# Two tile pools in place of one, the last operand pair built in steps, activations loaded by POOL's queue

## The chip, the cores and the metric

One core of a Trainium2 chip runs the whole program in one launch. The metric is device microseconds of that core, as the median of several runs. A profiled execution of the same kernel gives a trace; a difference of 0.2% (4.3 us here) is about what a measurement of this kernel can tell from no change.

## The reference

The program computes a small hybrid encoder on x of 1024 positions by 1024 channels in float32. It has two mixer layers, each followed by a gated feed-forward layer (FFN) of width 2816, and a last RMSNorm:

```python
for l in range(DEPTH):                       # DEPTH = 2
    h = rmsnorm(x, g_mix[l])
    if l % 2 == 0:                           # even mixer
        xa, ga, hb, bg, cg = jnp.split(h @ w_in_even[e], SPLIT_EVEN, axis=-1)
        xa = causal_dwconv(xa, lru_conv_w[e]) + lru_conv_b[e]
        ya = rg_lru(xa, ...) * jax.nn.gelu(ga)
        yb = bg * causal_dwconv(cg * hb, sconv_w[e])
        x = x + jnp.concatenate([ya, yb], axis=-1) @ w_out_even[e]
    else:                                    # odd mixer: pooling and HGRN2
        ...
        x = x + jnp.concatenate([yc, yd], axis=-1) @ w_out_odd[o]
    h = rmsnorm(x, g_ffn[l])
    u = causal_dwconv(h @ ffn_w_up[l], ffn_conv_w[l]) + ffn_conv_b[l]
    x = x + (jax.nn.gelu(u) * (h @ ffn_w_gate[l])) @ ffn_w_down[l]
return rmsnorm(x, g_final)
```

## The kernel before

**Numbers.** Every float32 operand of a large product is split into two parts that TensorE takes (`split`, L120: ScalarE, called ACT in the profile, writes the high part, VectorE, called DVE, the low part). Each product is then three matmuls: high·high, high·low, low·high. Channels lie on the 128 partitions, positions in the free dimension, so x is eight tiles of 128x1024 (512 KB).

**Stages.** The head (L644 to L696) loads x and the first weights channel block by channel block, multiplies them as they come, and takes the squares for the norm. `norm_cols` (L183) turns the sum of squares `ss` into a reciprocal root per position: eight small matmuls `pst`, a POOL power. `norm_bcast` (L196) spreads it over the partitions: DVE `dg`, the split `dh`, four matmuls `psb`, and the tile `rb`. The even mixer then runs 17 blocks of 48 matmuls (`block`, L143), each of which ends in an evacuation of its accumulator by DVE (`ev_ga` L598, `ev_hb` L613, `ev_cg` L619 and so on), and between them four chains of the linear recurrence. There are three such accumulators of two banks (pool `pm`) and two single banks (pool `pa`). `out_proj` (L518) multiplies by the output weights and hands each new x tile to `Entry.done` (L343).

**The FFN.** Up and gate products of one row tile of 128 channels are done together by `quad` (L287), a scheme with seven products in place of eight. Its products come in the order 1, 5, 6, 3, 7, 2, 4, each of 12 matmuls, on the banks X and ZY. Four weight sums per row tile (tiles `sa`, `sb`) are formed on POOL from the raw weights, split into `wh`, and used as the stationary operand. The other operands are 28 tiles `op`, seven products by four pairs of x tiles (j = 0 to 3; pair j is x[j] and x[j+4]). `build_ops` (L263) makes the seven of a pair when both are there; the out projection's order is (0,4,1), 5, 2, 6, 3, 7, so pair 3 comes last. The sum of squares for the FFN's norm is formed at the same time (`stat_add`, L175). `norm_cols` and `norm_bcast` run inside row tile 0, as hooks ahead of products 3 and 2.

There are 22 row tiles a layer. The gated result of tile f goes to DRAM (`asp[f]`). The down product loads it back in two chunks of k (11 and 11 tiles, or 9 and 9 with four left for `final_down` in the last layer): `load` (L379) by SP's queue into a tile `al`, and `halves` (L383) splits it into two tiles `a`.

**What sets the order.** The code is written in program order; a scheduler orders the instructions of each engine, and each engine runs its list strictly in order. SP issues all transfers, also in order: one that waits for its buffer holds all behind it. Tiles come from pools: `qp` with 41 buffers of 512 KB for x, halves, operands and temporaries alike, `rawp` with three raw weight buffers of 128x1024, `whp` with five split weight blocks.

Of the kernel before, what the change touches and what calls it, by code (L numbers as in the profile page):

```python
# [1 line left out]

# [1 line left out]

# [49 lines left out]
def trunk_kernel(ctx, tc, xT, wie, wout, wio, wv, wug, wdn, wgate, wpool, params, masks, pinv, yT):  # L54
    nc = tc.nc
    cpool = ctx.enter_context(tc.tile_pool(name="cpool", bufs=1))
    rawp = ctx.enter_context(tc.tile_pool(name="rawp", bufs=3))
    whp = ctx.enter_context(tc.tile_pool(name="whp", bufs=5))
    qp = ctx.enter_context(tc.tile_pool(name="qp", bufs=41))
    pm = ctx.enter_context(tc.tile_pool(name="pm", bufs=3, space=bass.MemoryType.PSUM))  # L60
    pa = ctx.enter_context(tc.tile_pool(name="pa", bufs=2, space=bass.MemoryType.PSUM))
    dp = ctx.enter_context(tc.tile_pool(name="dp", bufs=1, space=bass.MemoryType.DRAM))
# [133 lines left out]
    def norm_bcast(rc):  # L196

        dg = wtile("dg")
        V.tensor_tensor(dg[:, :S].rearrange("p (a b) -> p a b", b=P), ident[:, None, :].broadcast_to((P, 8, P)),
                        rc[:, :, None].broadcast_to((P, 8, P)), ALU.mult)  # L200
        dh = hltile("dh")
        split(dh, dg[:, :S])
        rb = cpool.tile([P, S], F32, tag="rb", name=uid("rb"))
        for hf in range(2):
            sl = slice(hf * 512, hf * 512 + 512)
            pb = pa.tile([P, 512], F32, tag="aux", name=uid("psb"))
            for b in range(2):
                T.matmul(pb, ones_r, dh[:, b, sl], start=(b == 0), stop=(b == 1))
            A.activation(rb[:, sl], pb, AF.Copy)
        return rb  # L210
# [49 lines left out]

    def build_ops(ops, j, lo, hi, g, g2):  # L263

        x11, x12, x21, x22 = lo[:, 0:512], lo[:, 512:S], hi[:, 0:512], hi[:, 512:S]
        ta, tb = wtile("ta"), wtile("tb")
        b12, n1, t2, t3 = ta[:, 0:512], ta[:, 512:S], tb[:, 0:512], tb[:, 512:S]
        stt = V.scalar_tensor_tensor

        def op(pr, src, gcol=None):  # L270
            ops[pr, j] = optile("op")
            split(ops[pr, j], src, gcol)

        op(1, x11, g)
        A.activation(b12, x12, AF.Copy, scale=g)
        stt(n1, x11, g, b12, ALU.mult, ALU.subtract)
        op(5, n1, -1.0)
        stt(t2, x22, g2, n1, ALU.mult, ALU.add)
        op(6, t2)
        op(3, x22, g2)  # L280
        stt(t3, x22, g2, b12, ALU.mult, ALU.subtract)
        op(7, t3)
        op(2, x21, g2)
        stt(t3, x21, g2, t2, ALU.mult, ALU.subtract)
        op(4, t3)

    def quad(w1, w2, np_, ops, fin, hooks=None):  # L287


        c = np_ * P  # L290
        raws = []
        for w in (w1, w2):
            raw = rawtile()
            nc.sync.dma_start(raw[:, :2 * c], w)
            raws += [raw[:, 0:c], raw[:, c:2 * c]]
        a11, a12, a21, a22 = raws
        sa, sb = wtile("sa"), wtile("sb")
        s1, s3, s2, s4 = sa[:, 0:c], sa[:, 512:512 + c], sb[:, 0:c], sb[:, 512:512 + c]
        G.tensor_tensor(s1, a21, a22, ALU.add)  # L299
        G.tensor_tensor(s3, a11, a21, ALU.subtract)  # L300
        G.tensor_tensor(s2, a22, s3, ALU.subtract)  # L301
        G.tensor_tensor(s4, a12, s2, ALU.subtract)  # L302
        X = pa.tile([P, 512], F32, tag="aux", name=uid("X"))
        ZY = pm.tile([P, 2, 512], F32, tag="ps", name=uid("ZY"))
        Z, Y = ZY[:, 0, :], ZY[:, 1, :]
        r1, g = wtile("r1"), wtile("g")

        def mm(pr, src, bank, first):
            if hooks and pr in hooks:
                hooks[pr]()  # L310
            wt = whp.tile([P, 2, 512], F32R, tag="wh", name=uid("wh"))
            split(wt[:, :, :c], src)
            for j in range(np_):
                for a, b in ((0, 0), (0, 1), (1, 0)):
                    T.matmul(bank, wt[:, a, j * P:j * P + P], ops[pr, j][:, b, :],  # L315
                             start=(first and j == 0 and a == 0 and b == 0), stop=(j == np_ - 1 and a == 1),
                             skip_group_check=not first)
# [16 lines left out]
    class Entry:
# [1 line left out]


        def __init__(self, l):
            self.l, self.n, self.x, self.ops = l, 0, {}, {}
            self.ss = wtile("ss")  # L340
            self.store = [dp.tile([P, S], F32, tag=f"xsd{l}_{n}", name=f"xsd{l}_{n}") for n in range(8)]

        def done(self, n, x):  # L343
            nc.sync.dma_start(self.store[n], x)
            self.x[n] = x
            j = n % 4
            if j in self.x and j + 4 in self.x:
                g, g2 = (pc("g_ffn", 8 * self.l + m) for m in (j, j + 4))
                build_ops(self.ops, j, self.x[j], self.x[j + 4], g, g2)
                for m in (j, j + 4):  # L350
                    stat_add(self.ss, self.n, self.x[m])
                    self.n += 1

    def ffn(l, ops, xsd, rb, hooks, last):
        asp = [dp.tile([P, S], F32, tag=f"asp{l}_{f}", name=f"asp{l}_{f}") for f in range(NF)]
# [2 lines left out]
        def up_gate(f):  # L358
# [12 lines left out]
                V.tensor_tensor(c, c, g, ALU.mult)  # L371
                nc.sync.dma_start(asp[f], c)

            quad(wug[l, 0, f], wug[l, 1, f], 4, ops, fin, hooks if f == 0 else None)

        for f in range(NF):
            up_gate(f)

        def load(src, s):  # L379
            t = wtile(s)  # L380
# [1 line left out]
            return t  # L382

        def halves(f):
            y = hltile("a")
            split(y, load(asp[f], "al"))
            return y

        f0 = 0
        for nk in CHUNKS[l]:  # L390
            ys = [halves(f) for f in range(f0, f0 + nk)]
            cols = slice(f0 * P, (f0 + nk) * P)
            parts = [4] * (nk // 4) + ([nk % 4] if nk % 4 else [])
# [661 lines left out]
```

## Time and profile before

| | us |
|---|---|
| median of 3 runs | 2140.82 (2138.69 to 2142.26) |
| profiled execution | 2139.35 |
| its span | 2137.6 |
| TensorE (PE) busy in it | 2067.8 |
| DVE busy | 1253.3 |
| ACT busy | 750.2 |
| POOL busy | 279.0 |

The profiled execution took 1.75 us more than its span and 1.47 us less than the median. In the timeline of an engine a row gives the start, the time that it covers, the engine, the line, and, in square brackets, how long the engine was idle before and what ended that. The FFN layers lie at about 354 to 1060 us and 1432 to 2137 us of the span, the even mixer with its head before, the odd mixer between.

### The profile page before, as it was taken

Reading aid. Unit: us, or ns where it says so; the run is one execution under the profiler, and the core shown is the slowest. Engines: PE = TensorE matmul, PEld = TensorE weight load, DVE = VectorE, ACT = ScalarE, POOL = GpSimd, SP = SyncE. Lnnn points to the kernel's source line nnn. Section 1 sums busy time; section 2 is a strip of 40 time slices with the busy share of each in tenths; the row PEclk is TensorE's granted clock in tenths of the full one; section 3 lists DMA queues with packets and bytes.
Section 4 is the critical chain, followed back from the end, with each engine's and each line's share of the span. In section 5 each row is a group of like instructions: output and inputs, shape, how many; then the busy total and the mean of one; then the engine's idle time right before and its main releaser. Section 6 shows DMA issues by size and latency. Waiting matters only on the chain.

```text
span 2137.6 us, 23850 instructions
## 1 busy us (share of the span) xinstructions
PE 2067.8 (97%) x9344; PEld 1695.1 (79%) x9344; DVE 1253.3 (59%) x1707; ACT 750.2 (35%) x1106; POOL 279.0 (13%) x208
## 2 busy tenths in 40 slices
PE   8999998999999999999999999989999999989998
PEld 6777886788888877888878887767888887778887
DVE  6655356666666673333536888766766676644325
ACT  5663133344433442221332121343433443323113
POOL 0000001322333220000000000012233223200002
PEclk9999999999999999999999999999999999999999
DMA  4111132122222225333210111332122222254212
GB/s 166 35 36 43 50 135 108 68 89 78 71 89 89 88 92 195 123 99 99 88 65 21 35 35 35 119 113 80 67 82 89 89 76 73 91 211 151 76 53 79
DMA packets 72448, 185.94 MB, mean 87 GB/s; under 512 B 7824, under 2 KB 17168, under 8 KB 72336
## 3 DMA queue, kind: packets, MB, share of 16 engines
q1 hardware_dynamic: 72336, 184.42, 25.1%
q8 instruction: 73, 1.20, 0.2%
q14 instruction: 39, 0.32, 0.0%
HBM read 144.55 MB, written 39.85 MB: 86 GB/s over the span
## 4 chain that ended last, share of the span: by engine, by line
PE 82%; issue 7%; DVE 5%; DMA 3%; ACT 3%; POOL 1%; SPq 0%; DVEq 0%; POOLq 0%; ACTq 0%
PE ps L167 40%; PE X L315 19%; PE ZY L315 16%; PE ps L430 2%; PE ps L975 2%; DMA al<-asp 1%; PE pl L843 1%; DMA x<-in_xT_dram 1%; DVE c L368 1%; DVE wh L124 0%; ACT c L366 0%; PE pg L579 0%; PE pp L942 0%; DVE ss L742 0%; ACT a L123 0%
## 5 line engine op out<-in xcount | busy, mean ns | idle before, releaser
L315 PE MATMUL X<-op,wh 128*128 128x512 f32 x2112 | 501.6, 389 | 0.0
L315 PEld LDWEIGHTS X<-op,wh 128*128 128x128 f32 x2112 | 396.7, 188 | 83.4 <-ACT wh L123 1.0
L167 PE MATMUL ps<-a,wh 128*128 128x512 f32 x1920 | 443.7, 393 | 14.4 <-ACT a L123 13.3
L167 PEld LDWEIGHTS ps<-a,wh 128*128 128x128 f32 x1920 | 362.4, 189 | 95.7 <-ACT a L123 16.1
L315 PE MATMUL ZY<-op,wh 128*128 128x512 f32 x1584 | 394.5, 396 | 18.7 <-ACT wh L123 16.6
L167 PE MATMUL ps<-h,wh 128*128 128x512 f32 x1584 | 381.4, 397 | 13.5 <-DVE ga L598 4.8
L123 ACT ACTIVATE wh<-raw 128x512 fp32r<-128x512 f32 x326 | 197.6, 606 | 545.7 <-PE ps L167 493.4
L124 DVE TENSOR_TENSOR wh<-raw,wh 128x512 fp32r<-128x512 f32 x326 | 211.6, 661 | 293.1 <-ACT wh L123 291.8
L315 PEld LDWEIGHTS ZY<-op,wh 128*128 128x128 f32 x1584 | 295.9, 189 | 93.9 <-ACT wh L123 17.4
L167 PEld LDWEIGHTS ps<-h,wh 128*128 128x128 f32 x1584 | 298.0, 190 | 76.4 <-issue 11.2
L366 ACT ACTIVATE c<-r,prm 128x1024 f32<-128x1024 f32 x44 | 50.7, 1152 | 396.6 <-issue 350.2
L299 POOL TENSOR_TENSOR sa<-raw 128x512 f32<-128x512 f32 x44 | 56.7, 1289 | 967.5 <-DMA raw<-in_wug_dram 549.4
L368 DVE SCALAR_TENSOR_TENSOR c<-r,prm,c 128x1022 f32<-128x1022 f32 x88 | 112.7, 1281 | 18.4 <-ACT c L366 18.3
L327 DVE TENSOR_TENSOR g<-X,g 128x512 f32<-128x512 f32 x44 | 30.4, 691 | 146.7 <-PE X L315 146.7
L124 DVE TENSOR_TENSOR a<-al,a 128x1024 fp32r<-128x1024 f32 x44 | 53.9, 1225 | 58.1 <-ACT a L123 57.9
L329 DVE TENSOR_TENSOR r<-ZY,r 128x1024 f32<-128x1024 f32 x44 | 53.9, 1225 | 43.5 <-PE ZY L315 43.5
L301 POOL TENSOR_TENSOR sb<-raw,sa 128x512 f32<-128x512 f32 x44 | 70.6, 1604 | 3.4
L123 ACT ACTIVATE a<-al 128x1024 fp32r<-128x1024 f32 x44 | 46.4, 1055 | 57.8 <-DMA al<-asp 52.7
L401 DVE TENSOR_TENSOR x<-x,ps 128x1024 f32<-128x1024 f32 x32 | 39.1, 1221 | 38.8 <-PE ps L167 38.6
L302 POOL TENSOR_TENSOR sb<-raw,sb 128x512 f32<-128x512 f32 x44 | 60.6, 1376 | 3.4
L300 POOL TENSOR_TENSOR sa<-raw,raw 128x512 f32<-128x512 f32 x44 | 60.3, 1371 | 0.0
L124 DVE TENSOR_TENSOR wh<-sa,wh 128x512 fp32r<-128x512 f32 x88 | 60.2, 684 | 0.0
(215 smaller groups left out, 2082.0 us busy)
## 6 DMA issues: line engine op xcount, KB each, us to landing
raw<-in_wug_dram SPq DMA_DIRECT2D x88, 512.0 KB, 4.7
asp<-c SPq DMA_DIRECT2D x44, 512.0 KB, 3.0
al<-asp SPq DMA_DIRECT2D x44, 512.0 KB, 3.6
raw<-in_wdn_dram SPq DMA_DIRECT2D x72, 256.0 KB, 2.7
raw<-in_wie_dram SPq DMA_DIRECT2D x34, 256.0 KB, 2.6
raw<-in_wout_dram SPq DMA_DIRECT2D x32, 256.0 KB, 2.6
xsd<-x SPq DMA_DIRECT2D x16, 512.0 KB, 2.9
x<-xsd SPq DMA_DIRECT2D x16, 512.0 KB, 5.7
```

The costliest lines, as they stand in the source:

```text
L123: A.activation(dst[:, 0, :], src, AF.Copy)
L124: V.tensor_tensor(dst[:, 1, :], src, dst[:, 0, :].bitcast(F32), ALU.subtract)
L167: T.matmul(ps[i][:, n, :], wt[:, a, c], rhs[k][:, b, n * 512:(n + 1) * 512], start=(k == 0 and a == 0 and b == 0), stop=(k == nk - 1 and a ...
L299: G.tensor_tensor(s1, a21, a22, ALU.add)
L300: G.tensor_tensor(s3, a11, a21, ALU.subtract)
L301: G.tensor_tensor(s2, a22, s3, ALU.subtract)
L302: G.tensor_tensor(s4, a12, s2, ALU.subtract)
L315: T.matmul(bank, wt[:, a, j * P:j * P + P], ops[pr, j][:, b, :], start=(first and j == 0 and a == 0 and b == 0), stop=(j == np_ - 1 and a ...
L329: V.tensor_tensor(r1, ZY.rearrange("p a b -> p (a b)"), r1, ALU.add)
L366: A.activation(c, u, AF.Identity, scale=pc("ffn_conv_w", base + 2 * NF))
L368: V.scalar_tensor_tensor(c[:, d:S], u[:, 0:S - d], pc("ffn_conv_w", base + (2 - d) * NF), c[:, d:S], ALU.mult, ALU.add)
L430: T.matmul(ps, wts[n // 2][:, a, o:o + P], ys[k][:, b, sl], start=(k == 0 and a == 0 and b == 0), stop=(k == nk - 1 and a == 1))
```

## The change

1. The pool `qp` of 41 buffers becomes two: `hp` (26) for split tiles, operands and loaded activations, and `wp` (15) for everything else. The operands of pair 3 for products 2 and 4, and `dh`, come from `wp`.
2. `rawp` has six buffers of 128x512 in place of three of 128x1024; a row tile's weights come in four transfers of 256 KB in place of two of 512 KB.
3. `build_ops` is cut into `build_lo`, which needs x[j] only, and the steps of `build_hi`. For pair 3 the steps run as hooks of row tile 0, each ahead of the product that needs it; the two norm functions move to the hooks ahead of products 7 and 4.
4. In row tile 0 the weight loads, POOL sums and splits are given a higher priority in the scheduler.
5. `halves` loads by POOL's queue into an `hp` tile and writes the low part over the loaded tile. In the last row tile it is called after each of the first six products.

```diff
-    rawp = ctx.enter_context(tc.tile_pool(name="rawp", bufs=3))
+    rawp = ctx.enter_context(tc.tile_pool(name="rawp", bufs=6))
-    qp = ctx.enter_context(tc.tile_pool(name="qp", bufs=41))
+    hp = ctx.enter_context(tc.tile_pool(name="hp", bufs=26))
+    wp = ctx.enter_context(tc.tile_pool(name="wp", bufs=15))
...
-        dh = hltile("dh")
+        dh = Pair(*(wp.tile([P, S], F32R, tag="w", name=uid("dh")) for _ in range(2)))
...
+    def op(ops, pr, j, src, gcol=None):
+        ops[pr, j] = optile("op", *((wp, "w") if pr in (2, 4) and j == 3 else (hp, "h")))
+        split(ops[pr, j], src, gcol)
+    def build_lo(ops, j, lo, g):
+        ta = wtile("ta")
+        b12, n1 = ta[:, 0:512], ta[:, 512:S]
+        op(ops, 1, j, lo[:, 0:512], g)
+        A.activation(b12, lo[:, 512:S], AF.Copy, scale=g)
+        V.scalar_tensor_tensor(n1, lo[:, 0:512], g, b12, ALU.mult, ALU.subtract)
+        op(ops, 5, j, n1, -1.0)
+        return b12, n1
+    def build_hi(ops, j, lo_, hi, g2):
...
+        def s6():
+            stt(t2, x22, g2, n1, ALU.mult, ALU.add)
+            op(ops, 6, j, t2)
...
+        return [s6, s3, s7, s2, s4]
...
+        early = tc.high_priority(offset=120) if hooks else nullcontext()
+        with early:
+            for w in (w1, w2):
+                for q in range(2):
+                    raws.append(rawtile()[:, 0:c])
+                    nc.sync.dma_start(raws[-1], w[:, q * c:(q + 1) * c])
...
+            with tc.high_priority(offset=60) if hooks else nullcontext():
+                wt = whp.tile([P, 2, 512], F32R, tag="wh", name=uid("wh"))
+                split(wt[:, :, :c], src)
...
+            if freed and pr != 4:
+                freed()
...
-            if j in self.x and j + 4 in self.x:
-                g, g2 = (pc("g_ffn", 8 * self.l + m) for m in (j, j + 4))
-                build_ops(self.ops, j, self.x[j], self.x[j + 4], g, g2)
+            if n < 4:
+                self.lo[n] = build_lo(self.ops, n, x, g)
+                self.stat(x)
+                return
+            steps = build_hi(self.ops, j, self.lo[j], x, g)
+            if j == 3:
+                self.rest = steps
+                return
...
         def halves(f):
-            y = hltile("a")
-            split(y, load(asp[f], "al"))
-            return y
+            al = hp.tile([P, S], F32, tag="h", name=uid("al"))
+            nc.gpsimd.dma_start(al, asp[f])
+            hi = hp.tile([P, S], F32R, tag="h", name=uid("a"))
+            A.activation(hi, al, AF.Copy)
+            V.tensor_tensor(al.bitcast(F32R), al, hi.bitcast(F32), ALU.subtract)
+            return Pair(hi, al.bitcast(F32R))
+        first = []
+        for f in range(NF):
+            up_gate(f)
...
-            ys = [halves(f) for f in range(f0, f0 + nk)]
+            ys = first + [halves(f) for f in range(f0 + len(first), f0 + nk)]
...
+        def last_stat():
+            s7()
+            entry.stat(entry.x[7])
+        def cols():
+            s2()
+            h1()
+        hooks = {5: s6, 6: s3, 3: last_stat, 7: cols, 2: s4, 4: h2}
```

**ACT at the entry of the first FFN.** Before, its list runs as follows. The operands `op_308` to `op_312` are pair 3's from x[7], `sq` are squares, `wh_324` is the first split of a POOL sum, for product 5.

```order
L123 ACTIVATE op_308_2343<-tb_305_2333 128x512
L126 ACTIVATE op_309_2346<-x_298_2269,prm_75 128x512
L123 ACTIVATE op_310_2350<-tb_305_2333 128x512
L126 ACTIVATE op_311_2353<-x_298_2269,prm_75 128x512
L123 ACTIVATE op_312_2357<-tb_305_2333 128x512
L180 ACTIVATE sq_313_2360<-x_292_2206 128x1024
L180 ACTIVATE sq_314_2363<-x_298_2269 128x1024
L123 ACTIVATE wh_324_2418<-sa_317_2392 128x512
L320 ACTIVATE r1_321_2400<-X_319_2398 128x512
L123 ACTIVATE wh_325_2434<-sb_318_2393 128x512
```

Now the first three splits of POOL sums, `wh_321` for product 5, `wh_323` for 6 and `wh_326` for 3, stand eight to ten rows above the fourth, `wh_332` for product 7, with which these rows begin. `op_299` and `op_300` are pair 3's from x[3], `op_320` to `op_324` those from x[7].

```order
L128 ACTIVATE wh_332_2483<-sa_313_2378 128x512
L128 ACTIVATE op_290_2203<-tb_285_2187 128x512
L131 ACTIVATE op_299_2273<-x_292_2209,prm_78 128x512
L131 ACTIVATE op_300_2278<-ta_298_2272 128x512
L348 ACTIVATE r1_317_2386<-X_315_2384 128x512
L128 ACTIVATE wh_334_2503<-raw_310_2372 128x512
L350 ACTIVATE g_318_2387<-ZY_316_2385 128x512
L128 ACTIVATE op_320_2405<-tb_308_2347 128x512
L131 ACTIVATE op_322_2424<-x_302_2284,prm_78 128x512
L128 ACTIVATE op_324_2444<-tb_308_2347 128x512
L185 ACTIVATE sq_325_2447<-x_302_2284 128x1024
L352 ACTIVATE r1_317_2386<-X_315_2384 128x512
```

The weight splits moved ahead of pair 3's operands, and these moved in between the evacuations of row tile 0.

**SP and POOL at the last row tile of the first FFN.** Before, SP's list is this; `raw` are down weights, `al` the activations, `asp0_21` the last row tile's store.

```order
L138 DMA raw_726_5586<-in_wdn_dram 128x512
L138 DMA raw_728_5615<-in_wdn_dram 128x384
L381 DMA al_679_5368<-asp0_0_2366 128x1024
L138 DMA raw_730_5639<-in_wdn_dram 128x384
L381 DMA al_682_5374<-asp0_1_2367 128x1024
L372 DMA asp0_21_2387<-c_676_5359 128x1024
L381 DMA al_685_5380<-asp0_2_2368 128x1024
```

Now the same loads stand in POOL's list, behind and between the four sums of the last row tile.

```order
L324 TENSOR_TENSOR sa_707_5327<-raw_705_5323,raw_706_5325 128x512
L325 TENSOR_TENSOR sa_707_5327<-raw_703_5319,raw_705_5323 128x512
L423 DMA al_714_5352<-asp0_0_2348 128x1024
L326 TENSOR_TENSOR sb_708_5328<-raw_706_5325,sa_707_5327 128x512
L327 TENSOR_TENSOR sb_708_5328<-raw_704_5321,sb_708_5328 128x512
L423 DMA al_717_5373<-asp0_1_2349 128x1024
L423 DMA al_720_5394<-asp0_2_2350 128x1024
L423 DMA al_723_5415<-asp0_3_2351 128x1024
```

The first load moved off SP's list to a place ahead of the last two sums; each load waits for the operand tile whose buffer it takes.

**DVE in the even mixer.** Before, `ga_113`, an evacuation that frees an accumulator, stands behind a chain of the recurrence (`gate`, `th`, `ya_107`).

```order
L592 TENSOR_TENSOR gate_102_664<-gate_102_664,th_105_675 128x1024
L593 SCALAR_TENSOR_TENSOR th_105_675<-gate_99_653,gate_102_664 128x1024
L606 TENSOR_TENSOR th_105_675<-th_105_675,ga_80_543 128x1024
L124 TENSOR_TENSOR wh_161_1088<-raw_160_1086,wh_161_1088 128x512
L124 TENSOR_TENSOR ya_107_688<-th_105_675,ya_106_687 128x1024
L598 TENSOR_TENSOR ga_113_750<-ps_108_691,rb_59_386 128x1024
```

Now:

```order
L632 TENSOR_TENSOR gate_102_667<-gate_102_667,xc_72_478 128x1024
L129 TENSOR_TENSOR ya_89_583<-th_87_570,ya_88_582 128x1024
L643 TENSOR_TENSOR ga_113_753<-ps_108_694,rb_59_389 128x1024
L129 TENSOR_TENSOR xch_98_653<-xc_96_647,xch_97_652 128x1024
L634 SCALAR_TENSOR_TENSOR th_105_678<-xc_72_478,th_105_678 128x1024
```

The evacuation moved from behind the second chain (`th_105`) to ahead of it, behind the first (`ya_89`). Likewise `p_158`, an evacuation (L619, now L664) that stood behind the fourth chain, stands behind the third. In the head, PE's list now has the eight `pst` behind 108 of the 144 matmuls and the four `psb` ahead of the last six; before, all twelve stand behind the 144.

More of the change, by code (lines that the diff above doesn't have):

```diff
@@ L1 @@
-from contextlib import ExitStack
+from contextlib import ExitStack, nullcontext
 import numpy as np
@@ L101, in wtile @@
     def wtile(s):
-        return qp.tile([P, S], F32, tag="q", name=uid(s))
+        return wp.tile([P, S], F32, tag="w", name=uid(s))
     class Halves:
         def __init__(self, s):
-            self.t = [qp.tile([P, S], F32R, tag="q", name=uid(s)) for _ in range(2)]
+            self.t = [hp.tile([P, S], F32R, tag="h", name=uid(s)) for _ in range(2)]
         def __getitem__(self, key):
@@ L115, in hltile, with __init__, optile @@
         return Halves(s)
-    def optile(s):
-        return qp.tile([P, 2, 512], F32R, tag="q", name=uid(s))
+    class Pair(Halves):
+        def __init__(self, *t):
+            self.t = t
+    def optile(s, pool, tag):
+        return pool.tile([P, 2, 512], F32R, tag=tag, name=uid(s))
     def split(dst, src, gcol=None):
@@ L133, in rawtile @@
     def rawtile():
-        return rawp.tile([P, S], F32, tag="raw", name=uid("raw"))
+        return rawp.tile([P, 512], F32, tag="raw", name=uid("raw"))
     def wunit(src, cols):
@@ L251, in small_tables @@
         return cc, ncc, lb, ol
[L263 to L267, printed above, removed]
-        stt = V.scalar_tensor_tensor
[L270 to L285, printed above, removed]
@@ new lines, in build_hi, with s3, s7, s2 @@
+    def build_hi(ops, j, lo_, hi, g2):
+        b12, n1 = lo_
+        x21, x22 = hi[:, 0:512], hi[:, 512:S]
+        tb = wtile("tb")
+        t2, t3 = tb[:, 0:512], tb[:, 512:S]
+        stt = V.scalar_tensor_tensor
+        def s6():
+            stt(t2, x22, g2, n1, ALU.mult, ALU.add)
+            op(ops, 6, j, t2)
+        def s3():
+            op(ops, 3, j, x22, g2)
+        def s7():
+            stt(t3, x22, g2, b12, ALU.mult, ALU.subtract)
+            op(ops, 7, j, t3)
+        def s2():
+            op(ops, 2, j, x21, g2)
+        def s4():
+            stt(t3, x21, g2, t2, ALU.mult, ALU.subtract)
+            op(ops, 4, j, t3)
+        return [s6, s3, s7, s2, s4]
@@ L290, in quad @@
+    def quad(w1, w2, np_, ops, fin, hooks=None, freed=None):
         c = np_ * P
         raws = []
[L292 to L300, printed above, removed]
@@ L372, in fin @@
                 nc.sync.dma_start(asp[f], c)
-            quad(wug[l, 0, f], wug[l, 1, f], 4, ops, fin, hooks if f == 0 else None)
-        for f in range(NF):
-            up_gate(f)
+            quad(wug[l, 0, f], wug[l, 1, f], 4, ops, fin, hooks if f == 0 else None,
+                 (lambda: first.append(halves(len(first)))) if f == NF - 1 else None)
         def load(src, s):
@@ L705, in h2 @@
             box["rb"] = norm_bcast(box["rc"])
-        return ffn(l, entry.ops, entry.store, lambda: box["rb"], {3: h1, 2: h2}, last)
+        s6, s3, s7, s2, s4 = entry.rest
+        def last_stat():
[5 more added lines that the diff above has]
+        hooks = {5: s6, 6: s3, 3: last_stat, 7: cols, 2: s4, 4: h2}
+        return ffn(l, entry.ops, entry.store, lambda: box["rb"], hooks, last)
     entry = Entry(0)
```

25 lines of the change are left out of this document (16 added, 9 removed).

## Prediction

> **What bounds the kernel now.** I read the page first, then the table of windows, then PE's waits.
>
> ```profile
> span 2137.6 us, 23850 instructions
> PE 2067.8 (97%) x9344; PEld 1695.1 (79%) x9344; DVE 1253.3 (59%) x1707; ACT 750.2 (35%) x1106; POOL 279.0 (13%) x208
> ...
> 0.00:60.00 60.00, 48.86 (x208) 38.04 (x209) 40.37 (x77) 33.09 (x41) 3.37 (x8) 0.91 0.44 148
> 60.00:353.00 293.00, 283.57 (x1234) 233.77 (x1233) 159.81 (x170) 123.55 (x150) 0.41 (x1) 0.98 0.20 70
> 353.00:390.00 37.00, 27.57 (x116) 21.22 (x115) 23.77 (x28) 13.96 (x22) 13.71 (x9) 0.86 0.11 43
> 390.00:785.00 395.00, 394.34 (x1723) 321.53 (x1722) 263.20 (x310) 159.92 (x252) 111.15 (x80) 1.00 0.23 82
> 1430.00:1470.00 40.00, 30.57 (x129) 23.52 (x128) 27.88 (x34) 18.67 (x29) 11.86 (x8) 0.87 0.11 40
> ...
> PE ZY L315 <- ACT wh L123: 16.6, 2, 8.3
> PE ps L167 <- ACT a L123: 13.3, 6, 4.4
> PE ps L167 <- DVE ga L598: 4.8, 1, 4.8
> PE ps L167 <- DVE p L619: 4.6, 1, 4.6
> PE ps L975 <- ACT wv L130: 2.0, 2, 1.1
> ```
>
> A window's row has its length, then the busy time of PE, PE's weight loads, DVE, ACT and POOL, then the granted clock, the DMA share and GB/s. PE is the bound: idle 69.8 us in all (2137.6 less 2067.8). In the row tiles it is full (394.34 of 395.00), so nothing done there can gain. The idle time lies in a few places, and there the granted clock is below 1, so part of PE's busy time is lost too. At full pace 12 matmuls start 2.72 us apart (787.73 and 790.45 below), 0.2267 us each.
>
> **The FFN entries.** PE, then ACT and POOL, in the timeline of before:
>
> ```profile
> 353.93 2.88 PE L315 MATMUL X<-op,wh 128*128 128x512 f32 x12
> 365.10 1.22 PE L315 MATMUL ZY<-op,wh 128*128 128x512 f32 x2 [8.29 <-ACT wh L123]
> 373.12 1.05 PE L190 MATMUL pst<-ones,ss 128*128 128x128 f32 x8
> 385.84 5.60 PE L315 MATMUL X<-op,wh 128*128 128x512 f32 x24
> 357.14 0.63 ACT L123 ACTIVATE op<-tb 128x512 fp32r<-128x512 f32 x1 [6.47 <-DVE tb L278]
> 364.44 0.61 ACT L123 ACTIVATE wh<-sa 128x512 fp32r<-128x512 f32 x1
> 352.59 1.29 POOL L299 TENSOR_TENSOR sa<-raw 128x512 f32<-128x512 f32 x1 [306.04 <-PE ps L167]
> ```
>
> Product 5 waits for a weight split that stands on ACT behind all of pair 3's operands and two squares. Row tile 0 goes from 353.93 to 388.72 (its last 12 matmuls are the second half of the 385.84 row, 2.72 us further), 34.8 us. Full pace would be 84 x 0.2267 = 19.0, plus twice 1.05 for `pst`, plus 4 x 0.23 for `psb`: 22.1. The excess is 12.7 us.
>
> Now POOL's sums and the first three splits are done within the output projection. Pair 3's operands are made at about 355.8 to 362 (by the durations above, from x[7]'s arrival at about 355.5), each ahead of its product: PE has 9 matmuls on X and 7 to 9 on ZY to do first. What is late next is the norm: x[7]'s square must be added, then `pst`, POOL's power, `dg`, `dh`, and only then `psb`, one product before the end.
>
> ```profile
> 377.54 2.30 DVE L199 TENSOR_TENSOR dg<-ident,rc 128x1024 f32<-128x1024 f32 x1 [1.76 <-POOL rc L193]
> 382.25 0.50 PE L208 MATMUL psb<-dh,ones_r 128*128 128x512 f32 x1 [0.76 <-DVE dh L124]
> ```
>
> From `pst` to `psb` there were 1.76 + 2.30 + some 2.3 of split, 6.4 us; two products cover 5.4 of it, and two further waits of 0.4 to 0.8 as in the row remain: I leave 2.4 us. The gain is 10.3 us a layer; the second FFN's window (1430:1470) has the same 8.3 us wait (16.6 in two). **20.6 us**; at least 16.6 if only the waits go, at most 25.4.
>
> **The down entries.**
>
> ```profile
> 787.73 2.88 PE L315 MATMUL ZY<-op,wh 128*128 128x512 f32 x12
> 790.45 2.88 PE L315 MATMUL X<-op,wh 128*128 128x512 f32 x12
> 797.74 7.18 PE L167 MATMUL ps<-a,wh 128*128 128x512 f32 x18 [4.41 <-ACT a L123]
> 808.04 7.33 PE L167 MATMUL ps<-a,wh 128*128 128x512 f32 x31 [0.30 <-DVE a L124]
> 1866.57 2.88 PE L315 MATMUL X<-op,wh 128*128 128x512 f32 x12
> 1883.87 21.47 PE L167 MATMUL ps<-a,wh 128*128 128x512 f32 x91 [0.30 <-DVE a L124]
> 782.00 10.83 SPq L138 DMA_DIRECT2D raw<-in_wdn_dram  x6
> 792.88 0.42 SPq L381 DMA_DIRECT2D al<-asp  x1
> al<-asp SPq DMA_DIRECT2D x44, 512.0 KB, 3.6
> ```
>
> SP issues the first `al` only at 792.88, behind six weight loads that wait for buffers. Between the last row tile's end (790.45 + 2.88) and 808.04 there are 14.7 us for 21 matmuls that take 4.8 at full pace: 9.95 us lost, and 9.65 in the second layer (14.42 less 4.76). The 18 matmuls in 7.18 us are at nearly half pace, after a wait of 4.4.
>
> Now POOL's queue issues six loads in the last row tile, 0.7 us after its start at the earliest, and goes on as buffers come free. The trace has no transfer on POOL's queue, so what one costs POOL, d, is unknown. At least it is nothing; the nearest upper row is SP's landing time, 3.6 us, if POOL were held until the data is there. Three things hang on d. The last row tile's third sum stands behind the first load:
>
> ```profile
> 769.54 1.78 POOL L301 TENSOR_TENSOR sb<-raw,sa 128x512 f32<-128x512 f32 x1
> ```
>
> It feeds product 6, due 2 x 2.72 = 5.44 us into the tile: 0.7 + d + 1.8 + 1.3 of split leaves d up to 1.6 free. The fourth load must be split (2.3 us, `a` 1.06 on ACT and 1.23 on DVE) when the tile ends after 19.0 us: 0.7 + 4d + 3.6 + 2.3, free up to d = 3.1. The eleventh is needed 144 matmuls later (32.6 us): free up to 4.1. I take d = 1, nearer to SP's own 0.42 us of issue, and leave 1 us a layer for waits in the last row tile: **17.6 us** (19.6 at most; with d = 3.6, 2 us of sums late and 2 of loads a layer, 11.6).
>
> [...]
>
> **The head.**
>
> ```profile
> 42.57 2.05 PE L190 MATMUL pst<-ones,ss 128*128 128x128 f32 x16 [0.51 <-DVE ss L181]
> 48.95 2.48 PE L208 MATMUL psb<-dh,ones_r 128*128 128x512 f32 x4 [4.32 <-ACT dh L123]
> 55.51 12.92 PE L167 MATMUL ps<-h,wh 128*128 128x512 f32 x48 [4.08 <-DVE xa L555]
> 32.20 0.43 SPq L652 DMA_DIRECT2D x<-in_xT_dram  x1
> ```
>
> Three waits sum to 8.9 us; `psb` loses 1.6 and the block of 48 loses 2.0 to the slow pace: 12.5. With six buffers SP issues the last x some 10 us before 32.20, and `pst` stands ahead of 36 of the 144 matmuls (8.2 us), which cover power, `dg` and `dh`. I take **10 us**, since the squares may be late; if DMA holds x back as before, 0 to 8.
>
> **The even mixer.**
>
> ```profile
> 123.60 12.31 PE L167 MATMUL ps<-h,wh 128*128 128x512 f32 x46 [4.85 <-DVE ga L598]
> 177.66 22.52 PE L167 MATMUL ps<-h,wh 128*128 128x512 f32 x89 [4.58 <-DVE p L619]
> 116.42 2.29 DVE L593 TENSOR_TENSOR_SCAN th<-gate,gate 128x1024 f32<-128x1024 f32 x1
> 122.24 1.22 DVE L598 TENSOR_TENSOR ga<-ps,rb 128x1024 f32<-128x1024 f32 x1
> ```
>
> PE stands 4.85 and 4.58 us for an accumulator whose evacuation waits on DVE behind a recurrence chain, and runs slowly after (46 matmuls in 12.31 for 10.43, 89 in 22.52 for 20.18). Both evacuations now stand ahead of that chain; the chain's ya results have the out projection's start as their deadline, over 100 us on. Of 13.6 us I take the two waits, **9.4 us**, and keep the slow pace against waits that I don't see; 0 to 13.6.
>
> **The rest.** The odd mixer's lists are nearly as before; its 2.0 us for `wv` go, since those loads no longer queue behind norm work: **2.0**. With 15 buffers the last outputs wait for stores:
>
> ```profile
> out_dram<-y SPq DMA_DIRECT2D x16, 256.0 KB, 2.3
> ```
>
> POOL's second y waits for the first store, and one DVE y for that: about **0.5 us lost** (0 to 3). The four weight transfers in place of two cost SP 0.33 us an issue, 0.7 more in a row tile of 19 us, beside PE.
>
> **Sum.** 20.6 + 17.6 + 10 + 9.4 + 2.0 - 0.5 = 59.1 us. 2139.35 - 59.1 = 2080.3 by the profiled execution, and 1.5 more to stand against the median: 2081.7.
>
> **Rivals.**
> - POOL's queue is dear, but less than 4.1 us a load: the down entries' gain shrinks or goes. 59.1 - 17.6, and up to 4 us lost in the last row tiles: 2099 to 2103. For it: four sums and eleven loads in one list, beside a DVE that is busy 67% in the row tiles (263.20 of 395). Against: POOL is idle over half of a row tile. [...]
> - Head and mixer keep their waits in other places, because PE's list is only re-cut: 59.1 - 19.4, about 2101. For it: a pool of 15 where 41 were, and every list there changed. Against: each freed evacuation has a block of 10.9 us to spare.
> - Slower: POOL's loads each hold their queue for long. The eleventh is late by 11d - 45 us a layer (0.7 + 11d + 3.6 + 2.3 less 51.7), against 42 us gained elsewhere. It decides from d = 6.0; at d = 7 it is 64 us lost, 2163.
> - The steps are reordered but the 15 buffers make PE wait as long as before: 2141.
>
> **How the numbers follow.** Forecast 0.64, dear queue 0.14, other waits 0.13, slower 0.06, no change 0.03. The forecast's own range is 2066 (all upper ends: 25.4 + 19.6 + 12.5 + 13.6 + 2 = 73, so 2068, and 1.6 of run spread) to 2095; with both middle rivals 2066 to 2106. About 0.2% is what a measurement of this kernel can tell from no change. Faster 0.91, same 0.03, slower 0.06.
>
> **What would show it.** In the changed kernel's trace: at the FFN entries no wait for `wh` over 1 us, and `psb` the longest wait; row tile 0 in some 24.5 us. At the down entries `al` on POOL's queue in the last row tile and no wait for `a` over 1 us. In the head `pst` near 34 and the next block from about 45. No wait for `ga` or `p`. It would be wrong if waits for `wh` appear in row tile 21, or if PE's idle time stays above 45 us.

## The result, and the profile after

The changed kernel takes **2103.29 us** (median, 2101.89 to 2104.02), beside 2140.93 for the kernel before on the same chip: a ratio of 0.982, 95% interval 0.981 to 0.984. The gain is 37.6 us where 59.1 were forecast, and the time lies above the forecast's own range (2066 to 2095). Its profiled execution took 2104.02 us, with a span of 2102.3.

The page of the changed kernel, with the rows that answer to those of before:

```profile
span 2102.3 us, 24201 instructions
PE 2058.6 (98%) x9344; PEld 1691.0 (80%) x9344; DVE 1280.6 (61%) x1707; ACT 745.6 (35%) x1106; POOL 341.8 (16%) x252
...
L423 POOL DMA_DIRECT2D al<-asp x44 | 23.7, 539 | 276.3 <-PE ps L172 207.3
...
al<-asp POOLq DMA_DIRECT2D x44, 512.0 KB, 6.7
```

PE's idle time fell from 69.8 to 43.7 us (2102.3 less 2058.6). DVE, with the same 1707 instructions, is busy for 1280.6 us in place of 1253.3: something makes its operations longer. A load on POOL's queue costs POOL 0.54 us, and its data is there after 6.7 us, where SP's took 3.6.

PE's waits now (what waits, for what; us in total, times, the longest):

```profile
PE ZY L341 <- DVE wh L129: 26.7, 37, 3.2
PE psb L213 <- DVE dh L129: 1.5, 2, 0.8
PE psb L213 <- ACT dh L128: 1.4, 2, 0.7
PE X L341 <- DVE op L132: 1.0, 2, 0.5
```

The waits of 8.3 us for ACT's `wh`, of 4.4 for `a`, of 4.8 for `ga` and 4.6 for `p` are gone. One has grown in their place, which before came 5 times, for 1.9 us in all: 37 waits of a row tile's product 5 for the low part of its `wh`, one in nearly every row tile. PE's timeline in the head and at the first FFN's entry:

```profile
32.38 1.95 PE L195 MATMUL pst<-ones,ss 128*128 128x128 f32 x16
44.06 11.18 PE L172 MATMUL ps<-h,wh 128*128 128x512 f32 x48 [0.58 <-DVE xa L600]
...
327.33 2.20 PE L341 MATMUL X<-op,wh 128*128 128x512 f32 x9
...
347.85 0.50 PE L213 MATMUL psb<-dh,ones_r 128*128 128x512 f32 x1 [0.69 <-ACT dh L128]
349.11 0.50 PE L213 MATMUL psb<-dh,ones_r 128*128 128x512 f32 x1 [0.76 <-DVE dh L129]
```

And the window of the steady row tiles of that layer (columns as in the prediction):

```profile
400.00:740.00 340.00, 332.59 (x1442) 269.06 (x1443) 234.39 (x261) 132.53 (x210) 106.33 (x66) 1.00 0.24 79
```

340 us for 1442 matmuls is 235.8 ns each; before it was 395 for 1723, 229.3 ns. The granted clock is 1.00 in both: PE stands, it isn't slowed. Following PE's first matmul of each stage through both traces, the span's 35.3 us divide so (the last digits are rounded):

| stage | forecast gain, us | measured gain, us |
|---|---|---|
| head and even mixer (first FFN begins at 327.33, before 353.93) | 19.4 | 26.6 |
| row tile 0 of both FFNs (25.39 for 34.63 in the first) | 20.6 | 18.5 |
| row tiles 1 to 20 of both (400.19 for 385.44; 400.38 for 386.39) | 0 | **-28.7** |
| row tile 21 and the first 21 down matmuls | 17.6 | 11.1 |
| rest of the down products | 0 | 3.0 |
| odd mixer | 2.0 | 4.0 |
| tail | -0.5 | 0.9 |

Of the 28.7 us, row tile 1 alone loses 10.6: it takes 24.51 and 24.48 us in the two layers, 19.18 in both before. Row tiles 2 to 20 lose 18.1.

**A steady row tile.** PE, DVE, POOL and SP's queue in the changed kernel:

```profile
444.71 3.27 SPq L320 DMA_DIRECT2D raw<-in_wug_dram  x4
446.42 0.69 DVE L129 TENSOR_TENSOR wh<-raw,wh 128x512 fp32r<-128x512 f32 x1 [1.19 <-ACT wh L128]
451.05 1.29 POOL L324 TENSOR_TENSOR sa<-raw,raw 128x512 f32<-128x512 f32 x1 [13.16 <-DMA raw<-in_wug_dram]
451.43 1.45 DVE L401 TENSOR_TENSOR g<-g,rb 128x512 f32<-128x512 f32 x1
...
453.43 1.23 DVE L357 TENSOR_TENSOR r<-ZY,r 128x1024 f32<-128x1024 f32 x1 [0.54 <-PE ZY L341]
454.11 1.29 POOL L326 TENSOR_TENSOR sb<-raw,sa 128x512 f32<-128x512 f32 x1
454.69 1.80 DVE L399 TENSOR_TENSOR r<-r,rb 128x1024 f32<-128x1024 f32 x1
455.48 2.17 POOL L327 TENSOR_TENSOR sb<-raw,sb 128x512 f32<-128x512 f32 x1
...
458.96 0.68 DVE L129 TENSOR_TENSOR wh<-sa,wh 128x512 fp32r<-128x512 f32 x1
459.69 0.50 PE L341 MATMUL ZY<-op,wh 128*128 128x512 f32 x1 [0.41 <-DVE wh L129]
```

SP's four loads were two and two: the third had to wait for the buffer that the split at 446.42 (of product 1 of the next row tile) gives back, and was issued at 447.18. So POOL's four sums start at 451.05 and lie beside DVE's work at the end of a row tile. `r*rb` (L399), 1.23 us when alone, takes 1.80; a sum, 1.29 alone, takes 2.17. DVE's list is then late by that, and in it the low part for product 5: PE waits 0.41 us.

**Row tile 1.** POOL, DVE and PE as row tile 1 begins:

```profile
351.53 1.29 POOL L324 TENSOR_TENSOR sa<-raw,raw 128x512 f32<-128x512 f32 x1
351.70 2.21 DVE L399 TENSOR_TENSOR r<-r,rb 128x1024 f32<-128x1024 f32 x1 [1.51 <-ACT rb L214]
357.76 1.75 DVE L129 TENSOR_TENSOR wh<-sa,wh 128x512 fp32r<-128x512 f32 x1
359.56 3.42 PE L341 MATMUL ZY<-op,wh 128*128 128x512 f32 x10 [3.17 <-DVE wh L129]
```

Here it is the other way round: the sums that begin at 351.53 are those of row tile 2, and they come early. The last of their narrow loads was issued at 348.24, so they follow row tile 1's own sums at once and lie beside all of DVE's work at the end of row tile 0. `r*rb` takes 2.21 us, the low part 1.75, and PE waits 3.17.

**The last row tile.**

```profile
754.06 0.76 POOL L423 DMA_DIRECT2D al<-asp  x1 [22.14 <-DVE g L400]
754.14 3.09 DVE L406 SCALAR_TENSOR_TENSOR c<-r,prm,c 128x1022 f32<-128x1022 f32 x1 [0.34 <-ACT c L404]
754.84 1.30 POOL L326 TENSOR_TENSOR sb<-raw,sa 128x512 f32<-128x512 f32 x1
...
756.22 2.13 POOL L327 TENSOR_TENSOR sb<-raw,sb 128x512 f32<-128x512 f32 x1
757.15 1.75 DVE L129 TENSOR_TENSOR wh<-sa,wh 128x512 fp32r<-128x512 f32 x1
...
758.95 3.42 PE L341 MATMUL ZY<-op,wh 128*128 128x512 f32 x10 [2.71 <-DVE wh L129]
```

POOL stood 22.14 us before the first load, which waits for an operand's buffer and went out 1.16 us after that row tile began (752.90). The last two sums stood behind it and then met DVE at its busiest moment. `c` took 3.09 us (1.28 alone), `wh` 1.75 (0.68 alone), and PE waited 2.71.

### The profile page after: what moved, and what is told of

Its sections match the earlier page's. It is cut to its first block, busy times and chain, and to the rows that moved or that the text cites. A ratio compares the mean times of both kernels' runs of the same rounds, so it can differ in the third digit from the quotient of the medians.

```text
span 2102.3 us, 24201 instructions
## 1 busy us (share of the span) xinstructions
PE 2058.6 (98%) x9344; PEld 1691.0 (80%) x9344; DVE 1280.6 (61%) x1707; ACT 745.6 (35%) x1106; POOL 341.8 (16%) x252
## 4 chain that ended last, share of the span: by engine, by line
PE 70%; issue 21%; DVE 5%; ACT 2%; POOL 1%; DMA 0%; SPq 0%; DVEq 0%; POOLq 0%; ACTq 0%
PE ps L172 43%; PE ZY L341 9%; PE X L341 8%; DVE c L406 3%; PE ps L1031 2%; ACT c L404 2%; PE ps L475 2%; PE ps L714 1%; DVE wh L129 1%; PE pl L899 1%; PE pg L624 1%; DVE r L399 0%; PE pl L874 0%; PE po L941 0%; PE pp L998 0%
## 5 line engine op out<-in xcount | busy, mean ns | idle before, releaser
L341 PE MATMUL ZY<-op,wh 128*128 128x512 f32 x1584 | 399.3, 397 | 26.9 <-DVE wh L129 26.7
L172 PE MATMUL ps<-a,wh 128*128 128x512 f32 x1280 | 394.5, 389 | 0.0
L172 PE MATMUL ps<-h,wh 128*128 128x512 f32 x1584 | 376.2, 393 | 0.6 <-DVE xa L600 0.6
L172 PEld LDWEIGHTS ps<-a,wh 128*128 128x128 f32 x1280 | 240.3, 188 | 49.9
L172 PE MATMUL ps<-al,wh 128*128 128x512 f32 x640 | 249.0, 389 | 0.0
L324 POOL TENSOR_TENSOR sa<-raw,raw 128x512 f32<-128x512 f32 x44 | 60.0, 1363 | 838.1 <-DMA raw<-in_wug_dram 756.5
L172 PEld LDWEIGHTS ps<-al,wh 128*128 128x128 f32 x640 | 120.1, 188 | 24.9
L327 POOL TENSOR_TENSOR sb<-raw,sb 128x512 f32<-128x512 f32 x44 | 92.2, 2094 | 3.4
L399 DVE TENSOR_TENSOR r<-r,rb 128x1024 f32<-128x1024 f32 x44 | 78.3, 1779 | 4.4 <-ACT rb L214 3.0
L325 POOL TENSOR_TENSOR sa<-raw,raw 128x512 f32<-128x512 f32 x44 | 74.9, 1702 | 0.0
L357 DVE TENSOR_TENSOR r<-ZY,r 128x1024 f32<-128x1024 f32 x44 | 53.9, 1225 | 31.8 <-PE ZY L341 31.8
L423 POOL DMA_DIRECT2D al<-asp x44 | 23.7, 539 | 276.3 <-PE ps L172 207.3
```

The costliest lines, as they stand in the source:

```text
L172: T.matmul(ps[i][:, n, :], wt[:, a, c], rhs[k][:, b, n * 512:(n + 1) * 512], start=(k == 0 and a == 0 and b == 0), stop=(k == nk - 1 and a ...
L399: V.tensor_tensor(u, u, r, ALU.mult)
```

## The experiments

**Whose is the loss in the row tiles?** Theory N: it is the narrow raw tiles, which bring the sums later. The changed kernel with wide raw tiles:

```diff
-    rawp = ctx.enter_context(tc.tile_pool(name="rawp", bufs=6))
+    rawp = ctx.enter_context(tc.tile_pool(name="rawp", bufs=3))
...
-                for q in range(2):
-                    raws.append(rawtile()[:, 0:c])
-                    nc.sync.dma_start(raws[-1], w[:, q * c:(q + 1) * c])
+                raw = rawtile()
+                nc.sync.dma_start(raw[:, :2 * c], w)
+                raws += [raw[:, 0:c], raw[:, c:2 * c]]
```

> The changed kernel with three raw buffers of 128x1024 and two weight loads a row tile, as before the change; all else stays. Theory N (narrow buffers: the third of the four loads waits for product 1's split, POOL's sums start 2.6 us later in the row tile and meet DVE's last instructions of the tile, both get slower, and the split for product 5 is late): no wait of ZY for a split in row tiles 2 to 20, and 19.27 us a row tile as before, 20 to 29 us less than the changed kernel; the head loses up to 11 us of its gain, since x waits for raw buffers again. Total 2075 to 2088. Theory W (the 15 buffers of wp, or DVE's new list, make DVE late in every row tile): row tiles stay at 19.9 us, total 2100 to 2115.

Measured: 2079.89 us, ratio 0.972 [0.971, 0.974]. First POOL and DVE in the timeline of a steady row tile of this kernel, then SP's queue in it a row tile on, then PE's wait for `wh`:

```profile
404.49 1.29 POOL L324 TENSOR_TENSOR sa<-raw 128x512 f32<-128x512 f32 x1 [13.59 <-DMA raw<-in_wug_dram]
...
408.80 1.30 POOL L327 TENSOR_TENSOR sb<-raw,sb 128x512 f32<-128x512 f32 x1
410.05 1.22 DVE L399 TENSOR_TENSOR r<-r,rb 128x1024 f32<-128x1024 f32 x1
...
419.32 0.92 SPq L319 DMA_DIRECT2D raw<-in_wug_dram  x2
```

```profile
PE ZY L341 <- DVE wh L129: 6.2, 4, 2.7
```

Both loads go out together, the sums end as `r*rb` begins, and it takes 1.22 us (1.30 in the mean of all 44, where the changed kernel has 1.78). 4 waits are left of 37, two of them the 2.7 us of the last row tiles. Row tile 1 takes 19.36 us again: the second weight of row tile 2 is loaded only at 360.58, so its sums begin at 364.19, behind DVE's work. The time is 23.4 us less than the changed kernel's.

The other way round, the kernel before with six narrow raw tiles and four loads, the same edit reversed:

```diff
-    rawp = ctx.enter_context(tc.tile_pool(name="rawp", bufs=3))
+    rawp = ctx.enter_context(tc.tile_pool(name="rawp", bufs=6))
...
```

> The kernel before with six raw buffers of 128x512 and four weight loads a row tile, and no other part of the change. Theory N: row tiles 1 to 20 of both layers get 0.5 to 0.8 us longer each, with PE waits of ZY for DVE's wh, 20 to 32 us in all; the head gets 8 to 13 us shorter; total 2145 to 2165. Theory W: row tiles stay at 19.27 us, total 2125 to 2141.

PE's new wait in it:

```profile
PE ZY L315 <- DVE wh L124: 19.9, 40, 1.4
```

Measured: 2161.66 us (one run), 22.1 more than before on that chip. The waits come with the narrow tiles, in a kernel that has nothing else of the change; and its head stays as it was (the block after `psb` at 56.26), where 8 to 13 us less were expected.

Are they too narrow or too few? The changed kernel with eight narrow raw tiles (and 14 buffers in `wp`, to make room):

```diff
-    rawp = ctx.enter_context(tc.tile_pool(name="rawp", bufs=6))
+    rawp = ctx.enter_context(tc.tile_pool(name="rawp", bufs=8))
-    wp = ctx.enter_context(tc.tile_pool(name="wp", bufs=15))
+    wp = ctx.enter_context(tc.tile_pool(name="wp", bufs=14))
```

> The changed kernel with eight raw buffers of 128x512 and 14 buffers in wp. Theory N: with eight, no load waits for product 1's split of the row tile ahead, the sums start early again, row tiles take 19.2 to 19.3 us and the head keeps its gain: 2070 to 2082. Theory W: with one buffer less in wp row tiles are at least as slow as in the changed kernel: 2103 to 2125.

Measured: 2083.45 us, 0.973 [0.972, 0.975]. Row tiles 2 to 20 take 19.18 to 19.84 us, most of them 19.2, so four loads cost nearly nothing there once the buffers let them go early. Row tile 1 keeps its whole loss (24.50 and 24.47 us, with waits of 3.2), as its neighbour's sums still come early. With the waits of the last row tiles this makes the time a little more than expected.

The wide tiles, with the first sum of each row tile but the first made three times, which moves the sums later and fills POOL:

```diff
+            for _ in range(0 if hooks else 2):
+                G.tensor_tensor(s1, a21, a22, ALU.add)
```

> As e1, with POOL's first sum of each row tile but the first done three times over (1.3 us each), so that the other sums start 2.6 us later though the weights are there. Theory N (what counts is when the sums run): row tiles of 19.8 us or more, 20 to 60 us above e1. If it is the loads themselves (four transfers, their landing) and not the time of the sums: as e1 within 3 us, since POOL is idle for more than half of a row tile. Theory W: as e1.

Measured: 2137.15 us (one run), 57 more than with wide tiles alone, with 40 waits for `wh` of 36.2 us in all. The edit does two things at once, so this doesn't yet tell late sums from sums in DVE's way.

**Late sums, or sums that hold DVE?** The sums could be late for their own splits, or it could be what they do to DVE. The changed kernel, with every engine's list in the same order in the trace, and one operand of L399 changed, from `rb` (SBUF) to the accumulator (PSUM):

```diff
-                V.tensor_tensor(u, u, r, ALU.mult)
+                V.tensor_tensor(u, u, ZY.rearrange('p a b -> p (a b)'), ALU.mult)
```

> The changed kernel as it is, six narrow raw tiles, and one operand different: L399 multiplies r by the accumulator ZY in PSUM in place of rb in SBUF, so the up result isn't normalized (the computation is another one there); every engine's list keeps its order. Theory C (POOL's late sums cost time because they meet DVE operations with both inputs in SBUF, and stretch them): r*ZY takes 1.23 us again in place of 1.8, the wait for wh in the steady row tiles shrinks from 0.4 to 0.6 us to under 0.2, row tiles 1 to 20 take 19.1 to 19.6 us in place of 20.0, time 2080 to 2094. Rival (the sums or their splits are simply late, however long DVE's operation takes): row tiles stay at 19.9 to 20.1 us, time 2100 to 2105.

Measured: 2073.39 us, 0.969 [0.967, 0.970]: 29.9 us less than the changed kernel. The window of its steady row tiles, then the group of L399 (busy us, mean ns, idle before), then POOL and DVE in the timeline of a row tile:

```profile
400.00:735.00 335.00, 335.00 (x1470) 274.18 (x1469) 226.20 (x260) 130.80 (x206) 92.00 (x66) 1.00 0.26 85
```

```profile
L399 DVE TENSOR_TENSOR r<-r,ZY 128x1024 f32<-128x1024 f32 x44 | 53.7, 1220 | 1.4
```

```profile
448.51 1.30 POOL L326 TENSOR_TENSOR sb<-raw,sa 128x512 f32<-128x512 f32 x1
448.96 1.22 DVE L399 TENSOR_TENSOR r<-r,ZY 128x1024 f32<-128x1024 f32 x1
449.88 1.29 POOL L327 TENSOR_TENSOR sb<-raw,sb 128x512 f32<-128x512 f32 x1
```

The sums still lie beside L399, and neither is longer than alone; PE is full, 227.9 ns a matmul. So the lateness of the sums costs nothing by itself. Row tiles 1 to 20 take 385.24 and 385.33 us, as in the kernel before; row tile 1 alone keeps 1.7 of its 5.3 us. So all of the row tiles' loss, more than the 2080 to 2094 of Theory C would give back, hangs on one DVE operation: with both inputs in SBUF, beside POOL's sums, it took 1.78 us in the mean, with one of them in PSUM 1.22.

**What did the pools do alone?** The kernel before with the two pools and nothing else:

```diff
-    qp = ctx.enter_context(tc.tile_pool(name="qp", bufs=41))
+    hp = ctx.enter_context(tc.tile_pool(name="hp", bufs=26))
+    wp = ctx.enter_context(tc.tile_pool(name="wp", bufs=15))
...
```

> The kernel before with the two pools alone (26 and 15 buffers, wide raw weight tiles, all of the FFN and its loads as before). Theory S (the pools let the scheduler put psb, ga and p earlier, and that alone gave the head and the even mixer their 26.6 us): the block after psb starts near 44 us in place of 55.5, the out projection near 327 to 329, no wait for ga or p above 1 us, time about 2114 (2110 to 2118). Rival (the weights in halves, or SP's queue without the activations, carried part of it): the block starts at 50 or later, or a wait of 4 us for ga or p stays, time 2122 to 2140.

PE's timeline in its head and at its first FFN's entry:

```profile
44.37 11.18 PE L172 MATMUL ps<-h,wh 128*128 128x512 f32 x48 [0.58 <-DVE xa L560]
...
327.70 2.20 PE L320 MATMUL X<-op,wh 128*128 128x512 f32 x9
334.68 0.49 PE L320 MATMUL X<-op,wh 128*128 128x512 f32 x1 [4.78 <-ACT op L131]
```

Measured: 2114.0 us (one run). The whole gain of the head and the mixer is the pools': the FFN begins at 327.70. But its entry is worse than before: PE waits 4.78 us for an operand and then 7.2 for `wh`, in each layer, and row tile 0 takes 39.87 and 40.49 us, where it took 34.63 and 34.65.

**What did the steps do?** The changed kernel with wide raw tiles, pair 3 built at x[7] all at once, and the norm functions at their old hooks:

```diff
-            if j == 3:
-                self.rest = steps
-                return
...
-        hooks = {5: s6, 6: s3, 3: last_stat, 7: cols, 2: s4, 4: h2}
+        hooks = {3: h1, 2: h2}
```

> The changed kernel with wide raw tiles, and pair 3's operands built at x[7] all at once instead of in steps; the norm goes back to the hooks of products 3 and 2. Theory H (the steps are what took the 8.3 us wait away): PE waits for the wh of product 5 behind pair 3's operands on ACT again, 7 to 8 us in each first row tile, and the norm's psb is late again: 2096 to 2104. Rival (the priority alone would do): the first row tiles stay at some 25 us, 2078 to 2084.

PE's two longest waits in it:

```profile
PE ZY L341 <- ACT wh L128: 12.4, 2, 6.2
PE X L341 <- ACT op L131: 8.8, 2, 4.4
```

Measured: 2108.05 us (one run), 28.2 more than with the steps, and above the 2096 to 2104 expected: the wait for `wh` came back, 6.2 us each where 7 to 8 were expected, and one for the operands themselves with it. `psb` waits no longer than in the changed kernel, which was not expected. 26.9 of the 28.2 lie in row tile 0 (39.35 and 38.37 us for 25.42 and 25.39). The higher priority alone doesn't prevent these waits.

**Is POOL's queue worth anything?** Three kernels with wide raw tiles. First, the same loads on SP's queue:

```diff
-            nc.gpsimd.dma_start(al, asp[f])
+            nc.sync.dma_start(al, asp[f])
```

> The changed kernel with wide raw tiles, and the activations loaded by SP's queue, at the places in the program where POOL issued them. Theory Q (POOL's own queue is worth something): SP's list holds the first loads behind waits for operand buffers and the down weights behind those, so the down product waits for a or wh again, 3 to 8 us a layer; against that the 2.7 us wait of the last row tile's product 5 goes, since no load stands ahead of the sums any more; 2079 to 2092. Rival (only the earlier call of halves counts, the queue is indifferent, and its place ahead of the sums even costs): 2070 to 2076.

Measured: 2068.19 us, 0.967 [0.965, 0.968]: 11.7 us less than on POOL's queue and below both expectations. Theory Q falls: loading by POOL's queue, as the changed kernel does it, was no gain but a cost. Then POOL's queue with the loads behind the sums:

```diff
+            if f == 0:
+                G.tensor_tensor(al.bitcast(F32R)[:, 0:64], gate["s4"][:, 0:64], gate["s4"][:, 0:64], ALU.add)
             nc.gpsimd.dma_start(al, asp[f])
```

> The changed kernel with wide raw tiles, and one small POOL operation that reads the last row tile's fourth sum and writes 64 columns of the first al, ahead of its load: it puts the loads behind all four sums. Theory L (the first load holds the last two sums, and its issue stretches a DVE operation to 3.1 us): the wait of 2.7 us for product 5 and the slow pace after it go in both layers, 7 to 9 us less than with wide raw tiles alone: 2071 to 2074. Rival (the loads come later now and the wait moves to the down product): 2077 to 2082, with a wait for a at its start.

DVE and POOL at its first load:

```profile
738.75 1.28 DVE L409 SCALAR_TENSOR_TENSOR c<-r,prm,c 128x1022 f32<-128x1022 f32 x1 [0.34 <-ACT c L407]
739.11 0.76 POOL L428 DMA_DIRECT2D al<-asp  x1 [0.31 <-POOL al L427]
```

Measured: 2073.11 us, 0.969 [0.968, 0.971]: 6.8 us less than with the sums behind the load. The 2.7 us wait is gone, and `c` takes 1.28 us with the load's issue beside it, so the issue did not stretch this operation, which had begun 0.36 us before it. Last, SP's queue without the early calls of `halves`:

```diff
-                 (lambda: first.append(halves(len(first)))) if f == NF - 1 else None)
+                 None)
```

> The run with wide raw tiles and SP's queue, and halves called after the last row tile again, as in the kernel before, with its tiles still from the pool of operands. Theory B (the loads come early because they go into buffers that the operands leave in the last row tile; the place of the call in the code matters little): the first loads are still issued within the last row tile, no wait for a or al above 1 us at the down product, 2067 to 2072. Rival (the early calls made the loads early): the waits of before return, 4.4 us and slow pace, 8 to 18 us for both layers: 2076 to 2086.

SP's queue in its last row tile, and the page's row on these loads:

```profile
738.02 1.69 SPq L423 DMA_DIRECT2D al<-asp  x2
```

```profile
al<-asp SPq DMA_DIRECT2D x44, 512.0 KB, 4.3
```

Measured: 2067.47 us, 0.966 [0.965, 0.968], the same as with the early calls. The first loads still go out within the last row tile, which ends at 756.32, since the buffers they wait for are the operands', which come free one after another there. With the two pools alone, where `al` comes from `wp`, the first load goes out only at 771.72, as the last row tile ends, and the wait of 4.4 for `a` stays. So it is the pool of `al` that makes the loads early, neither the call's place nor the queue. This is the best version of the study: 3.4% less time than before, where the changed kernel has 1.8%.

## Why the prediction came out as it did

The term that failed is the one put at nothing, the row tiles. The others came out near their size, for the most part by the mechanism given. 2103.29 us lies within 2066 to 2106 only because the two middle rivals reach there, and neither of them is what happened.

- **Head and even mixer: right in the main, too small.** `pst` at 32.38 (forecast near 34), the next block at 44.06 (from about 45), no wait for `ga` or `p`. I took 19.4 of at most 26.1 (12.5 and 13.6), leaving the slow pace after the waits out of the mixer's term. 26.6 was measured: the slow pace went with the waits, as the block of 48 shows, which takes 11.18 us at a granted clock of 1.00 in place of 12.92 at 0.86. The pools-only run shows that the pools alone did it. One reason given for the head was wrong: the six raw buffers don't bring the last x earlier. With them alone it is issued at 32.68 (32.20 before), with the pools alone at 16.77, with both at 12.42. Before, SP's list had loads of the block weights (L138) between those of x; with the pools they all stand behind x.
- **FFN entries: right for row tile 0.** 18.5 for 20.6, row tile 0 in 25.39 us for "some 24.5", and `psb`'s 0.76 the longest wait in it, as forecast. (Row tile 0 of before ended at 388.56: its last product is the first half of the row at 385.84, not the second, so the excess was 12.5 us a layer and not 12.7.) The run without steps confirms what makes it. Two things were not in the term: the pools alone make this entry 5.2 and 5.8 us worse, so the steps had that to win back too, and right behind it row tile 1 lost 5.3 us a layer.
- **Row tiles: the step that failed.** "In the row tiles it is full (394.34 of 395.00), so nothing done there can gain" was read as if nothing could lose either, and the narrow raw tiles were priced at SP's issue time, "0.7 more in a row tile of 19 us, beside PE". In its place stood this: six narrow buffers hold as many bytes as three wide ones, but the second weight's loads now wait for a split of the next row tile's product 1; so the sums move beside `r*rb`, DVE and POOL hold each other up, and PE's product 5 waits. That is 18.1 us in row tiles 2 to 20. In row tile 1 narrow loads bring the next sums early, into the same collision: 10.6. Together -28.7 us, more than the whole miss of 21.5 (59.1 less 37.6). The timeline of before had shown how near it was, in the last sum of a row tile and `r*rb`, one ending as the other begins:

```profile
462.83 1.23 DVE L329 TENSOR_TENSOR r<-ZY,r 128x1024 f32<-128x1024 f32 x1 [1.19 <-PE ZY L315]
462.88 1.29 POOL L302 TENSOR_TENSOR sb<-raw,sb 128x512 f32<-128x512 f32 x1
464.09 1.23 DVE L361 TENSOR_TENSOR r<-r,rb 128x1024 f32<-128x1024 f32 x1
```

- **Down entries: mechanism right, size off.** The waits for `a` went, but 11.1 us came in place of 17.6. I put the risk in d, POOL's time for one load, and took 1 us; it is 0.54. What cost was the place: two sums stand behind the first load, and these then met DVE. My check was of product 6, which the third sum feeds. The wait came a product earlier: product 5's sum was long done, but the low part of its `wh` stood on DVE behind `c`. "It would be wrong if waits for `wh` appear in row tile 21": they did, 2.71 and 2.57. (The other sign, idle time above 45 us, did not show: 43.7.) With wide raw tiles, the sums first were worth 6.8 us and SP's queue 11.7.
- **Two rivals have nearly the measured time**, and in both it agrees by chance. "POOL's queue is dear" (2099 to 2103) had the down entries' gain go and the rest stay; here nearly two thirds of that gain stayed and the row tiles lost. "Head and mixer keep their waits" (about 2101) had 19.4 us go that came in full.
- **The rest.** Odd mixer 4.0 for 2.0, rest of the down products 3.0 for nothing, tail 0.9 gained where 0.5 was to be lost. With the two pools alone the odd mixer gains 3.8 and the rest of the first down product 2.25, so these too are mostly the pools'; by what waits was not followed.

## What to carry to other kernels

A full engine can still lose: ask how much slack the work that feeds it has, and what a change moves beside that work, before putting a stage at nothing. When buffers are cut in two, count in which order the pieces come free, not how many bytes they hold. And a load on POOL's queue, ahead of two sums in POOL's list, held that list until its buffer was free (22.14 us here); put such a load on an engine's list behind what others wait for, or on another queue.

## What the runs showed of the hardware

**DVE and POOL hold each other up, to the hundredth.** In the rows above, `r*rb` begins at 454.69 while a sum runs until 455.40 (454.11 and 1.29), 0.71 us later; 1.80 less 0.71 is 1.09. The next sum begins at 455.48, DVE ends at 456.49, and the sum ends at 457.65, 1.16 after. I worked this out for the 17 row tiles between 395 and 714 us of the first layer in which L399 begins within a sum: its time less the rest of that sum is 1.07 to 1.09 in all, and the next sum ends 1.15 to 1.17 after DVE does, whether the operation took 1.50 or 2.29. The 6 of the 44 that lie beside no sum take 1.22 in the mean. I read this as neither being slowed, and each standing until the other is done; the trace has the times and not the cause. `g<-g,rb` (L401), with both inputs in SBUF too, takes 1.42 in the mean of the 33 that begin within a sum; the 7 that begin with a sum or ahead of it take 0.69, as without one, and there the sum takes 1.43 to 1.84. The operations of DVE that lie beside a sum with an accumulator in PSUM among their inputs (`r<-ZY,r`, `g<-X,rb`) keep their time: L357 has a mean of 1.225 us though 40 of its 44 lie beside one, and `g<-X,rb` takes 0.68 or 0.69 in all 38 that do. What makes one stand for the other was not shown.

**POOL's loads.** The issue of one took POOL 0.53 us in the median of the 44, and 0.53 in that of the 33 that lie beside a DVE operation too; the first of each layer took 0.76 and 0.62. The landing took 6.7 us in the changed kernel. On SP's queue the same loads took 3.6 in the kernel before, 4.3 in the last run and 6.2 with the two pools alone, so the queue is not shown to be what lengthens it, and no run shows one such load with nothing else in flight.

**Open.** The DVE operation of 3.09 us began at 754.14, 0.70 us before the sum behind the load began, and yet ended 1.09 us after that sum did (756.14). The second layer shows the same (2.94 us). That the load's issue, 0.08 us ahead of it (754.06), held something in these cases is my guess from the times and not shown; the 37 DVE operations that lie beside another issue and no sum took their usual time to 0.02 us. The loads on POOL's queue behind the sums are still 4.9 us behind those on SP's, where the 95% intervals of the two ratios just touch. 3.9 of it lie in the last row tiles (20.85 and 21.41 us for 19.17 in both layers), where PE waits 1.38 and 1.88 us for DVE's `g` ahead of product 4. What made `g` late was not followed.
